# Seven block products in another order: the second layer's down stage of a trunk kernel, with two weight sums by DMA and later weight loads

## The chip, the cores and the metric

The kernel runs on one core of a Trainium2 chip. The metric is the device time of one execution in microseconds. The kernel before was timed three times, the changed kernel is timed beside it.

## The reference

One sequence of 1024 tokens with 1024 channels goes through two layers in fp32. Each layer has a token mixer and a dense FFN, both behind an RMSNorm and an affine modulation, with a gate on the residual; one RMSNorm ends the stack.

```python
for i in range(DEPTH):                       # DEPTH = 2, D_FF = 2816
    mod = c_act @ ada_w[i] + ada_b[i]
    sh_m, sc_m, g_m, sh_f, sc_f, g_f = jnp.split(mod, N_ADA, axis=-1)
    h = modulate(rms_norm(x, norm_mix_g[i]), sh_m, sc_m)
    y = conformer_conv(...) if i % 2 == 0 else multiscale_pool(...)
    x = x + (1.0 + g_m)[:, None, :] * y
    h = modulate(rms_norm(x, norm_ffn_g[i]), sh_f, sc_f)
    y = (silu(h @ w_gate) * (h @ w_up)) @ w_down
    x = x + (1.0 + g_f)[:, None, :] * y
return rms_norm(x, final_g)
```

The change is in the last line but one of the second layer's FFN, the product with `w_down`, and in the final norm.

## The kernel before

**Numbers and tiles.** Activations lie with channels on the 128 partitions and tokens along the free axis, in two chunks A and B of 512 tokens. Every fp32 value is used as a pair of a rounded part and a rest ("hi", "lo"), and every product is three passes on TensorE (hi x hi, hi x lo, lo x hi). So a weight tile that comes in as `raw` needs a cast on ScalarE (`w<-raw`, CAST, the hi) and a subtraction on VectorE (`w<-raw,w`, the lo), and an operand block `op` likewise (`hi<-op`, `lo<-op,hi`). All vector, scalar and POOL arithmetic is recorded at line 126, all matmuls at line 148.

**Stages.** Layer 0 (convolution mixer, FFN), layer 1's pooling mixer, then layer 1's FFN. Gate and up run as eleven joint units (`joint`, line 1176) with one level of Strassen's block scheme: each unit needs sums of weight blocks, which are made by a load on SP (`raw<-in_wgu_dram`) and an accumulating DMA on POOL into the same tile (line 1108), or by subtractions on VectorE (`s<-raw,raw`). At its end a unit writes three operands `k` for the down stage to DRAM (`kinds<-k`, from `paired`, line 1232).

**The down stage** (`Seven`, lines 1480 and following; about 1500 to 1704 us). The product with `w_down` is cut in 2 x 2 blocks and done as seven block products p1 to p7. Each has parts q = 0 to 5, each part one weight tile of 128 x 1024 (q = 5 half as wide) and one operand; a whole part is 24 matmuls of 512 columns. Four PSUM banks gather a block product over its parts. The banks of "x" gather p1, then p6, p7 and p4 on top of it, and at the end of each some half of a chunk is complete and is added to the residual by four VectorE instructions (`x<-dn,gains,x`, the updates, line 1008). The banks of "y" gather p2's parts 4 and 5, and later p5 and p3. (p2's other parts are done elsewhere.) The table's columns are name, weight, operand, banks, whether the banks start fresh, which (chunk, half) is updated at the end, and the parts:

```python
("p2", "a12", "b21", "y", True, [(A, 0)], [4, 5]),
("p1", "a11", "b11", "x", True, [(A, 0)], every),
("p6", "s2", "t2", "x", False, [(B, 0)], every),
```

The weights a12, a11, a22 are plain loads of `in_wds_dram`. s1 and s2 come by a load and an accumulating DMA on POOL. s2 then subtracts a11, which p1 left in the block named `s`. s3 and s4 are a load followed by a subtraction on VectorE (`weights_of`, line 1426, its `load` and `halves`).

**Order.** TensorE's instructions stay in the order of the program. The other engines' and the queues' order is set by a scheduler that goes by its own estimates; an edge such as "behind the products" (`order`, line 150) only fixes a place in the queue and makes nothing wait on the chip. `Seven.run` emits a unit per part: first it loads the part four steps on, then it splits the part two steps on (cast and subtraction), then come the products, then the updates if the step ends. Loads go through SP in order: each part's weight and operand, and each waits for a free slot (five for raw weights, four for operands). The accumulations wait in POOL's queue.

**The end.** p3's last parts run in two halves of 256 token columns (`ending`), in whose shadow the norm of B's first half is made: a sum over partitions by matmuls (`var<-ones,acc`), eight tiny VectorE steps for the inverse root (`col`, `var`), a spread by matmul (`rstd<-ident,col`), scalings of x and output. Chunk A's final norm (`final`, line 1630) is a task that starts when p4 has ended and runs beside p5 and p3.

Of the kernel before, what the change touches and what calls it, by code (L numbers as in the profile page):

```python
# [12 lines left out]
AF = mybir.ActivationFunctionType  # L13
# [50 lines left out]
SPLIT = 2  # L64
# [67 lines left out]
def trunk(ctx, tc, xT, c, vec, ada, adan, w1f, w1, wdg, w2, wgu, wdn, wds, wpl, out):  # L132
# [526 lines left out]
    def unit(emit, *weights):  # L659
        units.append((weights, emit))  # L660
# [515 lines left out]
    def joint(l, fp, between=None):  # L1176
# [55 lines left out]
        def paired(i, f, g, u):  # L1232

            duo, k = kinds_d[l][fp // 2], c.setdefault("k", {})
            if i:
                if not k:
                    k[0] = block("u0", "k", F32)
                else:
                    k[1], k[2] = block("u0", "k", F32), block("u0", "k", F32)
                    sync.dma_start(k[2][:, 1], kept_d[l][fp // 2][:, fp % 2])  # L1240
                gated(l, i, f, g, u, into=k[0][:, 1 - f % 2])
                if 1 in k:
                    V_.tensor_tensor(k[1][:, 0], k[0][:, 1], k[0][:, 0], op=SUB)
            else:
                gated(l, i, f, g, u, into=k[2][:, 0])
                V_.tensor_tensor(k[1][:, 1], k[1][:, 0], k[2][:, 0], op=ADD)
                V_.tensor_tensor(k[2][:, 1], k[2][:, 1], k[1][:, 1], op=SUB)
                V_.tensor_tensor(k[0][:, 0], k[0][:, 1], k[1][:, 1], op=SUB)
                for b in (2, 1, 0):
                    soft.dma_start(duo[b][:, fp % 2], k[b])  # L1250

# [174 lines left out]
    def weights_of(l, kind, q):  # L1426

        n = duo_width(q) * 512
        src = lambda b: wds[q, b][:, :n]
        got = {}  # L1430

        def load():
            if kind == "a11":
                r = st["s2", q] = block("h0", "s", F32).rearrange("p a b -> p (a b)")[:, :n]
            else:
                r = raw_tile()[:, :n]
            first, *plus = {"a11": (0,), "a12": (1,), "a22": (3,), "s1": (2, 3), "s2": (2, 3), "s3": (3,), "s4": (1,)}[kind]
            nc.sync.dma_start(r, src(first))
            for b in plus:
                order(nc.gpsimd.dma_start(r, src(b), accum_op=ADD))  # L1440
                clock["G"] = max(clock["G"], clock["PE"]) + 0.9
            got["raw"] = r

        def halves():
            r = got["raw"]
            if kind in ("s2", "s3", "s4"):
                h = st["s2", q]
                to = r if kind == "s3" else h
                V_.tensor_tensor(to, r, h, op=SUB)
                r = to  # L1450
            wt = wts.tile([P, 2, D], F32R, tag="w", name=nm("w"))
            S_.copy(wt[:, 0, :n], r)
            V_.tensor_tensor(wt[:, 1, :n], r, wt[:, 0, :n].bitcast(F32), op=SUB)
            return wt

        return load, halves
# [23 lines left out]
    class Seven:  # L1480
# [24 lines left out]
        def run(self, after={}, ending=None):  # L1505
            for i, (name, key, fresh, ends, qs, q) in enumerate(self.steps):
                def emit(take, i=i, key=key, fresh=fresh, ends=ends, qs=qs, q=q):
                    self.load(i + LOADED + 1)
                    self.split(i + SPLIT + 1)
                    if key is None:  # L1510
                        return
                    if fresh and q == qs[0]:
                        self.banks[key] = [bank("dn") for _ in range(4)]
                    bs, (wt, ops) = self.banks[key], self.ready.pop(i)
                    for ds in ((0, 1), (2, 3)):
                        for j, g in enumerate(ops):
                            for d in ds:
                                last = q == qs[-1] and j == len(ops) - 1
                                products(bs[d], wt, 4 * j + d, g, fresh and q == qs[0] and j == 0, last, more=True)
                                if last:  # L1520
                                    for ch, half in ends:
                                        update(ch, 4 * half + d, bs[d], gate_f, self.l)
                            pace()
                unit(emit)
                if (name, q) in after:
                    after[name, q]()
            if ending is not None:
                unit(lambda take: ending([self.ready.pop(i) for i in sorted(self.ready)]))
# [99 lines left out]
        return upper, emit  # L1628

    def final(ch):  # L1630
        acc = yield from sum_sq(x[ch.i], ch.n)
        rstd = yield from mean_rsqrt(acc, ch.n, True, loose=True)
        for k in range(KT):
            xs = x[ch.i][k]
            V_.scalar_tensor_tensor(xs, xs, V("final_g", k), rstd, op0=MUL, op1=MUL)
            nc.sync.dma_start(out[:, k, ch.t0 : ch.t0 + ch.n], xs)
            yield
# [266 lines left out]
    def pool_end(ch):  # L1904
# [17 lines left out]
    every = list(range(NQ))  # L1922
    short = [q for q in every if q not in LAST]
    seven = Seven(1, [
        ("p2", "a12", "b21", "y", True, [(A, 0)], [4, 5]),
        ("p1", "a11", "b11", "x", True, [(A, 0)], every),
        ("p6", "s2", "t2", "x", False, [(B, 0)], every),
        ("p7", "s3", "t3", "x", False, [(B, 1)], every),
        ("p4", "a22", "t4", "x", False, [(A, 1)], every),
        ("p5", "s1", "t1", "y", True, [(B, 1)], every),  # L1930
        ("p3", "s4", "b22", "y", False, [(B, 0)], short),
        ("p3", "s4", "b22", None, True, [], LAST),
    ])
    all_joint(1, HEADS[1], between=seven.begin)
    upper, last_part = ending(B, 1)
    seven.run({
        ("p1", 0): lambda: unit(lambda take: x_in(B)),
        ("p4", NQ - 1): lambda: put("final_a", lambda: final(A)),
        ("p5", NQ - 1): lambda: unit(upper),
    }, last_part)  # L1940
    run_units(W_BUFS, early)

# [60 lines left out]
```

## Time and profile before

| | us |
|---|---|
| median of 3 runs | 1721.03 |
| lowest, highest | 1719.14, 1721.04 |
| profiled execution, its own time | 1717.94 |
| its span | 1716.1 |
| TensorE busy | 1676.0 (98%) |
| VectorE busy | 1321.6 (77%) |
| ScalarE busy | 795.3 (46%) |
| POOL busy | 475.7 (28%) |

The granted TensorE clock is 0.994 on average. The profile names instructions by tile (`out<-in`); an idle time in brackets is that of the engine just before the instruction, with what ended it. The profiled execution's own time lies 1.8 us above its span.

### The profile page before, as it was taken

The page shows a single profiled execution, that of the slowest core. Times are in us where ns is not written, and L with a number is a line of the kernel's source. Part 1 is how long each engine was busy: PE and PEld are TensorE (multiplying, and loading weights), DVE is VectorE, ACT ScalarE, POOL GpSimd, SP SyncE. Part 2 cuts the span into 40 slices and gives each one's busy share as a digit, 9 for nine tenths or more (in the row PEclk, how much of TensorE's full clock was granted, in tenths as well). Part 3 has the DMA queues.
Part 4 walks back from the last instruction along what each step waited for, and adds up shares of the span by engine and source line. Part 5 has one row for each costly group of instructions (what it writes and reads, how often), then busy time and mean ns, then how long its engine had stood idle before and what let it go on. Part 6 is the DMA issues. An engine that isn't in the chain of part 4 may idle for free.

```text
span 1716.1 us, 21376 instructions
## 1 busy us (share of the span) xinstructions
PE 1676.0 (98%) x7614; PEld 1362.7 (79%) x7614; DVE 1321.6 (77%) x1879; ACT 795.3 (46%) x1077; POOL 475.7 (28%) x561
## 2 busy tenths in 40 slices
PE   7999999999999999999999999999999999999987
PEld 5777777778887888888888888888788888878877
DVE  8889898898669797877665987868676767685485
ACT  3678686866546233233223437637222222233433
POOL 2588767795001121221110301101111111000101
PEclk9999999999999999999999999999999999999999
DMA  8958997737775888976876748868877777675851
GB/s 303 284 169 238 232 226 200 214 98 215 245 233 135 269 288 262 301 250 240 337 266 224 258 147 240 250 222 222 224 210 221 222 224 216 236 242 171 241 179 53
DMA packets 117613, 386.48 MB, mean 225 GB/s; under 512 B 12481, under 2 KB 14657, under 8 KB 117506
## 3 DMA queue, kind: packets, MB, share of 16 engines
q1 hardware_dynamic: 79680, 253.23, 42.1%
q0 software_dynamic: 36736, 130.83, 31.1%
q8 instruction: 60, 0.98, 0.2%
q10 hardware_dynamic: 1090, 1.05, 0.2%
q14 instruction: 47, 0.39, 0.1%
HBM read 317.69 MB, written 63.18 MB: 222 GB/s over the span
## 4 chain that ended last, share of the span: by engine, by line
PE 83%; DVE 5%; DMA 5%; issue 3%; POOL 1%; ACT 1%; DVEq 0%; POOLq 0%; ACTq 0%
PE dn L148 23%; PE a L148 22%; PE e L148 13%; PE p L148 9%; PE y L148 6%; PE g L148 3%; PE first L148 3%; PE tap L148 2%; DMA raw<-in_wds_dram 2%; DMA rd<-r 1%; POOL pa L126 1%; PE ada L148 1%; DMA s<-in_wds_dram 1%; DMA adaw<-in_adan_dram 1%; DVE t L126 1%
## 5 line engine op out<-in xcount | busy, mean ns | idle before, releaser
L126 ACT CAST w<-raw 128x1024 fp32r<-128x1024 f32 (+1 forms) x249 | 259.0, 1042 | 337.8 <-PE dn L148 97.7
L148 PE MATMUL dn<-g,w 128*128 128x512 f32 x1152 | 265.2, 391 | 1.7 <-DVE g L126 1.0
L126 DVE TENSOR_TENSOR w<-raw,w 128x1024 fp32r<-128x1024 f32 x177 | 217.9, 1234 | 52.7 <-ACT w L126 52.5
L148 PEld LDWEIGHTS dn<-g,w 128*128 128x128 f32 x1152 | 215.7, 188 | 47.6 <-DVE g L126 1.3
L148 PE MATMUL a<-n,w 128*128 128x512 f32 x1056 | 248.0, 390 | 1.2 <-DVE n L126 0.7
L148 PE MATMUL p<-h,w 128*128 128x512 f32 x1056 | 244.5, 391 | 1.7 <-ACT r L126 1.1
L126 POOL TENSOR_TENSOR pa<-pa,pr 128x512 f32<-128x512 f32 x160 | 227.6, 1507 | 23.4 <-ACT pr L126 17.1
L148 PEld LDWEIGHTS a<-n,w 128*128 128x128 f32 x1056 | 197.8, 188 | 44.6 <-DVE n L126 2.2
L148 PEld LDWEIGHTS p<-h,w 128*128 128x128 f32 x1056 | 197.2, 188 | 45.0 <-ACT r L126 2.3
L148 PE MATMUL dn<-hi,w 128*128 128x512 f32 (+1 forms) x600 | 177.4, 378 | 5.3 <-DVE x L126 5.3
L126 DVE SCALAR_TENSOR_TENSOR ca<-u,vecs,ca 128x512 f32<-128x512 f32 x245 | 169.7, 745 | 0.5
L126 DVE SCALAR_TENSOR_TENSOR x<-dn,gains,x 128x512 f32<-128x512 f32 (+1 forms) x140 | 98.4, 730 | 48.6 <-PE dn L148 48.6
L148 PEld LDWEIGHTS dn<-hi,w 128*128 128x128 f32 x600 | 111.0, 191 | 28.3 <-DVE x L126 7.2
L148 PE MATMUL a<-t,w 128*128 128x512 f32 x528 | 126.1, 395 | 4.6 <-DVE w L126 2.9
L148 PE MATMUL e<-b,w 128*128 128x512 f32 x528 | 123.4, 390 | 0.6 <-DVE r L126 0.6
L148 PE MATMUL e<-t,w 128*128 128x512 f32 x528 | 123.3, 389 | 0.0
L148 PEld LDWEIGHTS a<-t,w 128*128 128x128 f32 x528 | 100.5, 191 | 26.8 <-DVE w L126 3.8
L126 ACT ACTIVATE pr<-u,vecs 128x512 f32<-128x512 f32 x160 | 108.2, 716 | 24.3 <-POOL pa L126 18.8
L148 PEld LDWEIGHTS e<-b,w 128*128 128x128 f32 x528 | 99.1, 188 | 21.6 <-DVE r L126 1.0
L148 PEld LDWEIGHTS e<-t,w 128*128 128x128 f32 x528 | 99.1, 188 | 20.5
L1108 POOL DMA_DIRECT2D raw<-in_wgu_dram x41 | 36.3, 885 | 281.7 <-DVE k L126 88.3
L148 PE MATMUL dn<-lo,w 128*128 128x512 f32 (+1 forms) x300 | 112.9, 376 | 0.0
(179 smaller groups left out, 2371.3 us busy)
## 6 DMA issues: line engine op xcount, KB each, us to landing
raw<-in_wgu_dram SPq DMA_DIRECT2D x132, 512.0 KB, 5.1
adaw<-in_ada_dram POOLq DMA_DIRECT2D x48, 512.0 KB, 7.2
raw<-in_wdn_dram SPq DMA_DIRECT2D x44, 512.0 KB, 8.4
raw<-in_wgu_dram POOLq DMA_DIRECT2D x41, 512.0 KB, 7.1
raw<-in_w_dram SPq DMA_DIRECT2D x36, 512.0 KB, 6.3
gd<-g POOLq DMA_DIRECT2D x36, 512.0 KB, 7.8
g<-gd SPq DMA_DIRECT2D x36, 512.0 KB, 5.7
kinds<-k POOLq DMA_DIRECT2D x33, 512.0 KB, 7.2
```

The source lines that it names most:

```text
L126: self.last = self.order(getattr(self.eng, name)(out, *args, **kw))
L148: last_mm[0] = nc.tensor.matmul(out, lhsT, rhs, start=start, stop=stop, skip_group_check=more).ins.name
L1108: d = order(nc.gpsimd.dma_start(w[i], wgu[l, fp, src], accum_op=ADD))
```

## The change

1. The order of the steps. Before: p2, p1, p6, p7, p4, p5, p3. After: p2, p5, p1, p6, p7, p4, p3. p2 now gathers in "x" and p5 in "y" right behind it, and p5 serves both halves of B at its end (eight updates). p3 starts its banks afresh.
2. The sign of the operand t2 and of the weight sum s2 is turned. In `paired` two subtractions become additions and one addition becomes a multiply-and-subtract. s3 and s4 can then be sums: s3 is A22 loaded, with s2 accumulated by a POOL DMA from SBUF; s4 is A12 accumulated in place on s2 by a POOL DMA. Twelve VectorE subtractions go, and six more accumulating DMAs come.
3. All loads and accumulations of `in_wds_dram` get the edge behind the last product emitted (`placed`).
4. Chunk B's x is loaded block by block, one behind each of p5's first four parts. On the last part of a step the next split is emitted behind the updates.
5. Chunk A's final norm starts behind p7 with four of its squares; the rest waits until p4 has ended. The squares of B's upper half come behind p7 too.

```diff
-                V_.tensor_tensor(k[1][:, 1], k[1][:, 0], k[2][:, 0], op=ADD)
-                V_.tensor_tensor(k[2][:, 1], k[2][:, 1], k[1][:, 1], op=SUB)
-                V_.tensor_tensor(k[0][:, 0], k[0][:, 1], k[1][:, 1], op=SUB)
+                V_.scalar_tensor_tensor(k[1][:, 1], k[1][:, 0], -1.0, k[2][:, 0], op0=MUL, op1=SUB)
+                V_.tensor_tensor(k[2][:, 1], k[2][:, 1], k[1][:, 1], op=ADD)
+                V_.tensor_tensor(k[0][:, 0], k[0][:, 1], k[1][:, 1], op=ADD)
...
+        def placed(d):
+            if last_mm[0] is not None:
+                tc.add_manual_dep(d.ins, last_mm[0], edge, reason="behind the products")
+
+        def plus(r, what):
+            placed(nc.gpsimd.dma_start(r, what, accum_op=ADD))
+            clock["G"] = max(clock["G"], clock["PE"]) + 0.9
+
         def load():
+            if kind == "s4":
+                got["raw"] = st["s2", q]
+                plus(st["s2", q], src(1))
+                return
...
+            placed(nc.sync.dma_start(r, src({"a11": 0, "a12": 1, "a22": 3, "s1": 2, "s2": 2, "s3": 3}[kind])))
+            if kind in ("s1", "s2"):
+                plus(r, src(3))
+            elif kind == "s3":
+                plus(r, st["s2", q])
...
-            if kind in ("s2", "s3", "s4"):
+            if kind == "s2":
                 h = st["s2", q]
-                to = r if kind == "s3" else h
-                V_.tensor_tensor(to, r, h, op=SUB)
-                r = to
+                V_.tensor_tensor(h, h, r, op=SUB)
+                r = h
...
                     self.load(i + LOADED + 1)
-                    self.split(i + SPLIT + 1)
+                    if key is None or q != qs[-1]:
+                        self.split(i + SPLIT + 1)
...
+                    self.split(i + SPLIT + 1)
...
     def final(ch):
-        acc = yield from sum_sq(x[ch.i], ch.n)
+        acc = temp(ch.n, "acc", 2)
+        for k in range(KT):
+            while k == KT // 2 and "a_done" not in st:
+                yield "wait"
...
-        ("p2", "a12", "b21", "y", True, [(A, 0)], [4, 5]),
+        ("p2", "a12", "b21", "x", True, [(A, 0)], [4, 5]),
+        ("p5", "s1", "t1", "y", True, [(B, 1), (B, 0)], every),
...
-        ("p1", 0): lambda: unit(lambda take: x_in(B)),
-        ("p4", NQ - 1): lambda: put("final_a", lambda: final(A)),
-        ("p5", NQ - 1): lambda: unit(upper),
+        **{("p5", m): lambda m=m: unit(lambda take: x_in(B, m)) for m in range(KT // 2)},
+        ("p7", NQ - 1): final_begins,
+        ("p4", NQ - 1): lambda: unit(lambda take: st.__setitem__("a_done", True)),
```

**Place 1: POOL's queue at the start of the second layer's joint stage.** The difference of the two orders; `raw_12285`, `raw_12321` and `raw_12357` are weights of p6, the others belong to the joint stage and its normed inputs.

```order
 L488 DMA w_9751<-in_wgu_dram 128x1024
-L1440 DMA raw_12285<-in_wds_dram 128x1024
 L1096 DMA w_9852<-raw_9842 128x1024
-L1440 DMA raw_12321<-in_wds_dram 128x1024
 L165 DMA kept_4_203<-t_9880 128x512
-L1440 DMA raw_12357<-in_wds_dram 128x1024
 L165 DMA kept_4_203<-t_9947 128x512
 L1096 DMA w_9919<-raw_9844 128x1024
```

The three accumulations stood between the joint stage's own; now none of the down stage's is here. On SP the five loads that stood here (these three and p2's two) are gone as well.

**Place 2: weights that need a load and an accumulation.** SP's queue before, at p5's loads (`raw_12909` to `raw_13017` are the weights of p5's parts 0 to 3, `op_12912` to `op_12984` its operands 0 to 2, `op_12876` is p4's last operand):

```order
L1438 DMA raw_12909<-in_wds_dram 128x1024
L158 DMA op_12876<-kinds_5_2_222 128x512
L1438 DMA raw_12945<-in_wds_dram 128x1024
L158 DMA op_12912<-kinds_0_0_205 128x2x512
L1438 DMA raw_12981<-in_wds_dram 128x1024
L158 DMA op_12948<-kinds_1_0_208 128x2x512
L1438 DMA raw_13017<-in_wds_dram 128x1024
L158 DMA op_12984<-kinds_2_0_211 128x2x512
```

SP's queue now, at p7's loads (`raw_12713` to `raw_12823` are the weights of its parts 0 to 3, `op_12753` to `op_12854` its operands 1 to 4):

```order
L158 DMA op_12753<-kinds_1_1_209 128x2x512
L1449 DMA raw_12713<-in_wds_dram 128x1024
L158 DMA op_12790<-kinds_2_1_212 128x2x512
L1449 DMA raw_12750<-in_wds_dram 128x1024
L158 DMA op_12826<-kinds_3_1_215 128x2x512
L1449 DMA raw_12787<-in_wds_dram 128x1024
L158 DMA op_12854<-kinds_4_1_218 128x2x512
L1449 DMA raw_12823<-in_wds_dram 128x1024
```

A weight of part n stood behind the operand of part n-2; now it stands behind that of part n+1. VectorE's order now at the end of p6 (`w_12792`, `w_12844`, `w_12856` are the low halves of p7's weights 0 to 2; `dn_12438` to `dn_12441` are p6's four banks):

```order
L126 TENSOR_TENSOR w_12792<-raw_12713,w_12792 128x1024
L126 TENSOR_TENSOR lo_12796<-op_12716,hi_12795 128x1024
L126 TENSOR_TENSOR w_12844<-raw_12750,w_12844 128x1024
L126 TENSOR_TENSOR lo_12848<-op_12753,hi_12847 128x1024
L126 TENSOR_TENSOR w_12856<-raw_12787,w_12856 128x1024
L126 SCALAR_TENSOR_TENSOR x_12247<-dn_12438,gains,x_12247 128x512
L126 TENSOR_TENSOR lo_12860<-op_12790,hi_12859 128x1024
L126 SCALAR_TENSOR_TENSOR x_12247<-dn_12439,gains,x_12247 128x512
```

Before, the same rows stood there in the same way, but with weights that were one load each and a subtraction. The updates stand behind the low half of the next step's third weight in both.

**Place 3: VectorE at the end.** Now (`var_13541` and `col_13544` are the root of the ending's first half, `ny_13566` is A's spread root, `x_12285<-dn_13580` and `x_12285<-dn_13606` are the last two updates):

```order
L126 SCALAR_TENSOR_TENSOR var_13541<-col_13544 128x2
L126 SCALAR_TENSOR_TENSOR x_10797<-x_10797,vecs,ny_13566 128x512
L126 SCALAR_TENSOR_TENSOR x_10989<-x_10989,vecs,ny_13566 128x512
L126 SCALAR_TENSOR_TENSOR x_11181<-x_11181,vecs,ny_13566 128x512
L126 SCALAR_TENSOR_TENSOR col_13544<-var_13541,col_13544 128x2
L126 SCALAR_TENSOR_TENSOR x_10989<-x_10989,vecs,ny_13566 128x512
L126 SCALAR_TENSOR_TENSOR x_11181<-x_11181,vecs,ny_13566 128x512
L126 SCALAR_TENSOR_TENSOR x_10797<-x_10797,vecs,ny_13566 128x512
L126 SCALAR_TENSOR_TENSOR x_11373<-x_11373,vecs,ny_13566 128x512 x2
L126 SCALAR_TENSOR_TENSOR x_12285<-dn_13580,gains,x_12285 128x256
```

Before, the same place held only the root's steps and the last two updates (`x_12244<-dn_13588` and the next); A's eight scalings stood inside p3's first parts.

More of the change, by code (lines that the diff above doesn't have):

```diff
@@ L1436, in load @@
                 r = raw_tile()[:, :n]
[L1437 to L1441, printed above, removed]
+            placed(nc.sync.dma_start(r, src({"a11": 0, "a12": 1, "a22": 3, "s1": 2, "s2": 2, "s3": 3}[kind])))
[3 more added lines that the diff above has]
+                plus(r, st["s2", q])
             got["raw"] = r
@@ L1630, in final @@
     def final(ch):
-        acc = yield from sum_sq(x[ch.i], ch.n)
+        acc = temp(ch.n, "acc", 2)
+        for k in range(KT):
+            while k == KT // 2 and "a_done" not in st:
+                yield "wait"
+            sq = temp(ch.n) if k else acc
+            S_.activation(sq, x[ch.i][k], AF.Square)
+            if k == KT - 1:
+                V_.scalar_tensor_tensor(acc, sq, EPS_SUM, acc, op0=ADD, op1=ADD)
+            elif k:
+                V_.tensor_tensor(acc, acc, sq, op=ADD)
+            yield
         rstd = yield from mean_rsqrt(acc, ch.n, True, loose=True)
@@ L1929, in trunk @@
         ("p4", "a22", "t4", "x", False, [(A, 1)], every),
-        ("p5", "s1", "t1", "y", True, [(B, 1)], every),
-        ("p3", "s4", "b22", "y", False, [(B, 0)], short),
+        ("p3", "s4", "b22", "y", True, [(B, 0)], short),
         ("p3", "s4", "b22", None, True, [], LAST),
@@ L1935, in trunk, with final_begins @@
     upper, last_part = ending(B, 1)
+    def final_begins():
+        put("final_a", lambda: final(A))
+        unit(upper)
     seven.run({
-        ("p1", 0): lambda: unit(lambda take: x_in(B)),
-        ("p4", NQ - 1): lambda: put("final_a", lambda: final(A)),
-        ("p5", NQ - 1): lambda: unit(upper),
+        **{("p5", m): lambda m=m: unit(lambda take: x_in(B, m)) for m in range(KT // 2)},
+        ("p7", NQ - 1): final_begins,
+        ("p4", NQ - 1): lambda: unit(lambda take: st.__setitem__("a_done", True)),
     }, last_part)
```

## The prediction

> **What bounds the kernel now.** I read the page's first part, then a table of stretches, then the idle times of TensorE (PE) in the timeline, then what VectorE (DVE) and the DMAs did just ahead of each.
>
> ```profile
> PE 1676.0 (98%) x7614; PEld 1362.7 (79%) x7614; DVE 1321.6 (77%) x1879; ACT 795.3 (46%) x1077; POOL 475.7 (28%) x561
> ```
>
> TensorE is the bound. The change takes no product away, so it can only win where TensorE stands idle or runs at a lower clock, and lose where it makes such places. The stretches (columns: from:to, length, busy time and count of PE, PEld, DVE, ACT, POOL, granted clock, DMA share, GB/s):
>
> ```profile
> 1220.00:1250.00 30.00, 26.05 (x105) 20.77 (x104) 25.32 (x30) 9.66 (x11) 2.54 (x4) 0.89 0.70 218
> 1250.00:1280.00 30.00, 30.00 (x134) 24.86 (x133) 21.30 (x27) 8.12 (x9) 4.31 (x6) 1.00 0.74 210
> 1510.00:1515.00 5.00, 2.26 (x10) 1.43 (x8) 5.00 (x6) 3.91 (x5) 0.00 (x0) 0.96 0.85 294
> 1515.00:1520.00 5.00, 4.53 (x15) 3.25 (x14) 5.00 (x7) 0.94 (x1) 0.88 (x1) 0.70 0.82 248
> 1545.00:1550.00 5.00, 5.00 (x24) 4.12 (x23) 4.01 (x5) 1.34 (x2) 0.00 (x0) 1.00 0.39 138
> 1655.00:1660.00 5.00, 4.11 (x18) 3.45 (x19) 3.30 (x11) 0.00 (x0) 0.00 (x0) 0.79 0.30 105
> 1660.00:1665.00 5.00, 5.00 (x25) 4.21 (x24) 1.33 (x2) 1.57 (x2) 0.00 (x0) 0.86 0.00 0
> ```
>
> An undisturbed stretch does 134 products in 30 us, 0.224 us each, and 24 of them, one part of the down stage, in 5.4 us. TensorE's idle times, in brackets with the releaser:
>
> ```profile
> 1223.59 0.73 PE L148 MATMUL a<-t,w 128*128 128x512 f32 x2 [1.73 <-ACT w L126]
> 1226.54 7.46 PE L148 MATMUL a<-t,w 128*128 128x512 f32 x22 [2.22 <-DVE w L126]
> 1514.18 0.50 PE L148 MATMUL dn<-hi,w 128*128 128x512 f32 x1 [2.74 <-DVE x L126]
> 1515.98 0.79 PE L148 MATMUL dn<-hi,w 128*128 128x512 f32 x1 [0.47 <-DVE x L126]
> 1639.01 0.50 PE L148 MATMUL dn<-hi,w 128*128 128x512 f32 x1 [1.45 <-DVE x L126]
> 1655.89 1.05 PE L148 MATMUL var<-ones,acc 128*128 128x1 f32 x8 [2.31 <-DVE acc L126]
> 1672.51 0.47 PE L148 MATMUL dn<-hi,w 128*128 128x512 f32 x1 [0.62 <-DVE x L126]
> ```
>
> The first two are in the joint gate/up stage, the others in the second layer's down stage: the end of p2, the end of p4, the final norm of chunk A inside p5, and p5's end. The stretches add what the lower clock cost behind them.
>
> **The four waits of the down stage.** *End of p2.* DVE's timeline, then the chain of waits:
>
> ```profile
> 1506.50 1.22 DVE L126 TENSOR_TENSOR w<-s,w 128x1024 fp32r<-128x1024 f32 x1 [3.69 <-ACT w L126]
> 1513.38 0.75 DVE L126 SCALAR_TENSOR_TENSOR x<-dn,gains,x 128x512 f32<-128x512 f32 x1
> 1494.48 14.51 DMA s<-in_wds_dram
> ```
>
> The x update that frees the banks stood from 1511 to 1513.38 behind p1's weight work, which came late because its load took 14.51 us. The stall cost 2.74 + 0.47 us idle, plus 5 x (0.04 + 0.30) = 1.7 us of clock: 4.9. Counted the other way, 14 + 9 products missing against 24 per stretch, 23 x 0.224 = 5.2. I take 5.0. After the change p2 is followed by p5, which writes into fresh banks of its own, so TensorE need not wait for the x updates there until p1, six parts later. What remains is the third p5 weight, w_12212, queued on DVE ahead of p2's updates, and its load plus accumulation fall into DMAs that are still full. That costs 0 (the four x blocks of B no longer load here) to 3 (loads as slow as above); I take 0.5.
>
> *End of p4* (old place of the subtractions for s4):
>
> ```profile
> 1631.72 1.23 DVE L126 TENSOR_TENSOR s<-raw,s 128x1024 f32<-128x1024 f32 x1 [3.60 <-DMA raw<-in_wds_dram]
> 1636.47 1.23 DVE L126 TENSOR_TENSOR s<-raw,s 128x1024 f32<-128x1024 f32 x1 [0.32 <-DMA raw<-in_wds_dram]
> 1638.21 0.74 DVE L126 SCALAR_TENSOR_TENSOR x<-dn,gains,x 128x512 f32<-128x512 f32 x1
> ```
>
> The subtractions wait for their load, and the updates stand behind them. With s4 summed by DMA they are gone, and the step behind p4 is now p3 with weights long loaded: 1.5 us gained. In all, twelve subtractions leave DVE (ten of 1.23, two half as wide, about 13.6 us busy), but DVE is at 77% and elsewhere this is off the path: 0. The turned sign swaps one DVE form for another of nearly the same length, 0.
>
> *Final norm of A in p5.* Its matmuls stood in TensorE's order before their sum was ready: 2.31 us idle, 5 x (0.21 + 0.14) = 1.75 us of clock, 0.35 for the var matmuls themselves: 4.4. They now stand inside the ending, where the squares are long done: 4.4 gained. *1672.51*: the updates stood behind A's eight scalings; these move: 0.6. Together 5.0 + 1.5 + 4.4 + 0.6 = **11.5 gained**.
>
> *A rule against this arithmetic.* The rows show a granted clock of 0.70 and 0.79 behind idle times of 2.74 and 2.31 us. The Trainium skill ("TensorE: Matmul & The Clock Gate", Part 1) puts the drop behind an idle window of about 3.4 us. By that rule no clock would come back or be lost: 3.2 + 1.5 + 2.3 + 0.6 = 7.6 gained here, some 2.5 in the joint stage, 5.9 and 3.7 lost below, a net of -0.5 us, 1720.5. The granted clocks in these rows do not agree, so it gets no chance of its own beside R2, which ends near it, and I keep 11.5.
>
> **The joint stage.** Loads and accumulations of wds are now queued behind products, so three accumulations leave POOL's queue around 1177 to 1199, and five loads leave SP's. What followed there, on DVE and in the chain:
>
> ```profile
> 1210.93 10.23 DMA raw<-in_wgu_dram
> 1221.19 1.23 DVE L126 TENSOR_TENSOR s<-raw,raw 128x1024 f32<-128x1024 f32 x1 [4.88 <-DMA raw<-in_wgu_dram]
> ```
>
> DVE waited 4.88 us for an accumulation that POOL could issue only at 1210.93 and that took 10.23 us; TensorE then lost 1.73 + 2.22 idle and 30 x 0.11 = 3.3 of clock, 7.2 (by count 29 x 0.224 = 6.5; I say 7). Without the three transfers ahead of it I expect it 3 to 5 us earlier, with 4 needed. Range 0 to 7, taken **4.5 gained**. Those loads land in the down stage instead, where they are priced next.
>
> **New waits at the ends of p1 and p6.** p6 and p7 now both need a load and then an accumulation for every weight. SP's queue now has the load of part n behind the operand of part n+1, which waits for the lo of part n-3 to free its slot (before, p5's load stood behind the operand of part n-2). At the end of p1 and of p6, the x updates stand on DVE behind the weight of the next step's third part, so a late weight holds TensorE there. Nothing in the trace is exactly this; p5 before shows the pieces (DVE, SPq, SPq, POOL):
>
> ```profile
> 1606.94 1.22 DVE L126 TENSOR_TENSOR lo<-op,hi 128x1024 fp32r<-128x1024 f32 x1
> 1608.19 0.53 SPq L158 DMA_DIRECT2D op<-kinds  x1
> 1609.32 0.33 SPq L1438 DMA_DIRECT2D raw<-in_wds_dram  x1
> 1616.84 0.86 POOL L1440 DMA_DIRECT2D raw<-in_wds_dram  x1 [1.55 <-DVE lo L126]
> ```
>
> lo to operand 1.25 us, operand to load 1.13, then the latency L of load and accumulation, then the cast and the low half, 1.04 and 1.23 by the rows of the page and of DVE: three parts take 4.6 + L at least, and TensorE takes 3 x 5.4 = 16.3 for them. L has these bounds (the DMAs of 1540 to 1590 and of 1599 to 1630, and the page's):
>
> ```profile
> L126 ACT CAST w<-raw 128x1024 fp32r<-128x1024 f32 (+1 forms) x249 | 259.0, 1042 | 337.8 <-PE dn L148 97.7
> raw<-in_wds_dram SPq DMA_DIRECT2D x5, 512.0 KB, 5.1
> raw<-in_wgu_dram POOLq DMA_DIRECT2D x41, 512.0 KB, 7.1
> raw<-in_wds_dram SPq DMA_DIRECT2D x5, 512.0 KB, 7.4
> raw<-in_wds_dram POOLq DMA_DIRECT2D x5, 512.0 KB, 9.1
> 1599.00:1629.00 30.00, 30.00 (x133) 24.60 (x132) 14.72 (x16) 12.33 (x15) 4.32 (x5) 1.00 0.98 264
> ```
>
> Calm, L = 5.1 + 7.1 + 0.5 (POOL's issue behind the landing) = 12.7: 17.3 against 16.3, 1 us per three parts. Loaded, as in p5 before at a DMA share of 0.98, L = 17: 21.6 against 16.3, 5.3 per three parts. Up to p7's third part there are nine parts, three such rounds: 3 to 16 us, plus about 1.7 of clock per long stall. Fewer transfers are in flight now than in that p5, since loads are issued later, so I take the quarter next to calm, L = 13.5: 1.8 x 3 + about 1.1 of clock = 6.5, nearly all at the end of p6. Range 0 to 19. With the 0.5 from above, **7.0 lost**.
>
> One sentence by a page: the Trainium skill ("DMA: Bandwidth & Descriptors", Anatomy of one DMA) fits a POOL-issued DMA as 2.0 us plus its bytes at 436 GB/s, an estimate of 3.2 us for 512 KB, with which L would be 8.8 and this loss zero. The 7.1 and 9.1 of the trace do not agree with it.
>
> **The tail.** A's eight scalings now stand on DVE inside the root of the ending's first half and ahead of the last two x updates. TensorE runs that half's rstd before the last half's var.
>
> ```profile
> 1665.70 5.39 DVE L126 SCALAR_TENSOR_TENSOR x<-x,vecs,ny 128x512 f32<-128x512 f32 x8 [0.21 <-ACT ny L126]
> 1704.14 0.48 DVE L126 SCALAR_TENSOR_TENSOR x<-dn,gains,x 128x256 f32<-128x256 f32 x1 [1.67 <-PE dn L148]
> 1708.12 0.68 PE L148 MATMUL rstd<-ident,col 128*128 128x128 f32 x4 [1.74 <-DVE col L126]
> ```
>
> They cost 5.39 us; DVE's idle 1.67 ahead of the last update covers a part: **3.7 lost**, between 2.5 (more gaps are used) and 5.4 (none is). In the middle of a step, where they were, they cost only the 0.6.
>
> **Sum.** -11.5 - 4.5 + 7.0 + 3.7 = -5.3 us. The profiled execution took 1717.94 us (span 1716.1), 3.1 below the median of 1721.03, so its own time would become 1712.6, and on the median's scale **1715.7**.
>
> **Rivals.** *R1, the loads keep up* (L below 11.7, so 4.6 + L stays under 16.3, and the whole 7 of the joint stage comes back): -11.5 - 7 + 3.7 = -14.8, 1706.2. For it: 1545 to 1550 has a DMA share of only 0.39. Against: an accumulation took 7.1 even at the usual load. The page's fit for POOL's DMAs would lead here. Chance 0.20.
>
> *R2, the gains are eaten* (the accumulation of 1210.93 still lands late, since four copies with accumulation stay ahead of it on POOL, and L is 14: 2.3 x 3 + 1.7 + 0.5 = 9.1): -11.5 + 9.1 + 3.7 = +1.3, 1722.3. For it: 10.23 us for that one transfer is little touched by what POOL did 12 us earlier. Against: the loads that shared the engines are gone too. Chance 0.17.
>
> *R3, slower* (chained weights run at p5's latencies, L = 17: 16 us at the ends of p1 and p6, two clock drops 3.4, 0.5): -11.5 - 4.5 + 19.9 + 3.7 = +7.6, 1728.6. It decides against the change from 4.6 + L = 19.7, L about 15. For it: p6 and p7 now move a load, an operand and an accumulation per part, just as the 0.98 stretch does. Against: in that stretch TensorE stayed 30.00 of 30.00 us busy, and a stalled TensorE lets the transfers catch up. Chance 0.17.
>
> **How the numbers follow.** About 0.2% (3.4 us) can be told from no change, so faster means below 1717.6 and slower above 1724.5. The forecast's case (1711 to 1719) has 0.46, of which 0.39 is faster and 0.07 within. Faster: 0.39 + 0.20 = 0.59; same: 0.07 + 0.17 = 0.24; slower: 0.17. The range leaves out the half of R1 below 1706 and the half of R3 above 1728: 1706 to 1728. The likeliest case's own range is 1711 to 1719.
>
> **What would show it.** Right: no idle time of PE at p2's end, behind p4 and inside the down stage's last third; A's scalings as rows near the end, the last x update some 4 us behind its products and the last rstd some 4 us behind that update, as now; PE waiting for x at the end of p6 for 3 to 5 us, with DVE waiting for a DMA into raw ahead of it; 1220 to 1250 with over 120 products. Wrong: accumulations in p6 and p7 that land in under 6 us (R1), 1220 to 1250 still with some 105 (R2), or several stalls of over 4 us with loads and accumulations of 7 and 9 us (R3). A stall in p5's first parts would say that the weight sums can't follow p2 that fast.

## The result and the profile after

The changed kernel takes 1729.87 us (median of 4 runs, 1729.20 to 1731.55), the kernel before 1720.22 (1719.14 to 1721.04) beside it: a ratio of 1.0058, 95% interval 1.0041 to 1.0075. It is slower by 10 us, where 5 us less was forecast, and above the range of 1706 to 1728. The profiled execution took 1729.20 us, its span 1727.2, 11.1 more than before.

TensorE's work is the same, and so it is only where it stands still that has changed. The page's line, then five stretches:

```profile
PE 1678.7 (97%) x7614; PEld 1364.6 (79%) x7614; DVE 1311.0 (76%) x1871; ACT 795.7 (46%) x1077; POOL 484.2 (28%) x573
```
```profile
1220.00:1250.00 30.00, 30.00 (x134) 24.80 (x133) 26.40 (x33) 10.53 (x12) 3.35 (x5) 1.00 0.62 200
1570.00:1575.00 5.00, 1.41 (x3) 0.83 (x3) 3.81 (x5) 2.94 (x3) 0.86 (x1) 0.55 0.97 215
1575.00:1580.00 5.00, 4.92 (x18) 3.82 (x18) 4.78 (x6) 1.05 (x1) 0.00 (x0) 0.77 0.89 236
1610.00:1615.00 5.00, 4.45 (x10) 3.11 (x11) 5.00 (x7) 1.34 (x2) 0.75 (x1) 0.52 1.03 177
1645.00:1650.00 5.00, 4.43 (x11) 3.05 (x12) 2.54 (x3) 1.91 (x3) 0.00 (x0) 0.55 1.02 386
```

The joint stage is whole again, 134 products where there were 105. Three stretches of the down stage do 3 to 11 products where 24 fit. TensorE's idle times there, in its timeline:

```profile
1508.92 0.50 PE L148 MATMUL dn<-hi,w 128*128 128x512 f32 x1 [1.41 <-DVE x L126]
1573.59 0.77 PE L148 MATMUL dn<-hi,w 128*128 128x512 f32 x1 [6.12 <-DVE x L126]
1610.47 0.77 PE L148 MATMUL dn<-hi,w 128*128 128x512 f32 x1 [4.72 <-DVE x L126]
1645.06 0.47 PE L148 MATMUL dn<-hi,w 128*128 128x512 f32 x1 [2.12 <-DVE x L126]
```

These are the ends of p2, p1, p6 and p7. Summing by how much the start-to-start times of the down stage's products exceed their usual 0.2265 us gives what each place cost, clock included, and I use this count from here on. The sixteen small products of A's norm, which both kernels run, are left out of it:

| us lost | p2's end | p5's end | p1's end | p6's end | p7's end | p4's end | A's norm | sum |
|---|---|---|---|---|---|---|---|---|
| before | 5.1 | 0.9 | - | - | - | 1.7 | 4.2 | 11.9 |
| after | 2.8 | - | 8.3 | 7.3 | 6.3 | - | - | 24.7 |

From its first to its last product the down stage takes 203.4 us before (1500.4 to 1703.8) and 215.5 after (1496.5 to 1712.0), 12.1 more; 24.7 - 11.9 is 12.8. From the last product to the end it was 12.3 us and is 15.2. The joint stage brought 7 us; in this profiled execution 3 of them were lost again at 1131 us, where TensorE waited 2.1 us for ScalarE (0.9 before) and ran at a granted clock of 0.80 to 0.85 for the next few us. In the experiments' profiles with the same edge the down stage starts at 1493.1 to 1494.5.

**The wait at p1's end, followed back.** VectorE, SP's and POOL's queue of the changed kernel, then the DMAs of 1545 to 1605:

```profile
1564.61 1.23 DVE L126 TENSOR_TENSOR w<-s,w 128x1024 fp32r<-128x1024 f32 x1 [1.19 <-ACT w L126]
1569.15 1.22 DVE L126 TENSOR_TENSOR s<-s,raw 128x1024 f32<-128x1024 f32 x1 [2.18 <-DMA raw<-in_wds_dram]
1571.56 1.23 DVE L126 TENSOR_TENSOR w<-s,w 128x1024 fp32r<-128x1024 f32 x1 [1.19 <-ACT w L126]
1572.70 0.74 DVE L126 SCALAR_TENSOR_TENSOR x<-dn,gains,x 128x512 f32<-128x512 f32 x1
```
```profile
1550.23 0.55 SPq L1449 DMA_DIRECT2D raw<-in_wds_dram  x1
1558.93 0.87 POOL L1437 DMA_DIRECT2D raw<-in_wds_dram  x1 [1.36 <-DMA raw<-in_wds_dram]
```
```profile
raw<-in_wds_dram SPq DMA_DIRECT2D x9, 512.0 KB, 7.8
raw<-in_wds_dram POOLq DMA_DIRECT2D x5, 512.0 KB, 7.5
raw<-s POOLq DMA_DIRECT2D x3, 512.0 KB, 8.1
```

p1's last product began at 1567.1. Its updates stood behind the low half of p6's third weight (1571.56), whose load was issued at 1550.23, whose accumulation at 1558.93, and which could be used at 1569.15: L = 18.9 us. The five whole weights of p6 took 13.8, 14.9, 18.9, 17.5 and 11.7 us from load to landing, 15.4 in the mean. TensorE itself did not need the third weight yet: the low half of the second was done at 1565.8 and that of the third at 1572.8, and without the wait p6's second part would have begun at about 1572.8 and its third at 1578.2 (parts of 5.4 us behind 1567.3).

**The wait at p7's end** was not foreseen. Here p4's weights are single loads. POOL's queue, ScalarE and VectorE, and the DMAs of 1620 to 1642:

```profile
1620.40 2.12 POOL L1437 DMA_DIRECT2D s<-in_wds_dram  x2
1624.13 0.88 POOL L1437 DMA_DIRECT2D s<-in_wds_dram  x1 [1.61 <-PE dn L148]
1630.53 0.86 POOL L1437 DMA_DIRECT2D s<-in_wds_dram  x1 [5.53 <-issue]
```
```profile
1640.54 1.05 ACT L126 CAST w<-raw 128x1024 fp32r<-128x1024 f32 x1 [4.90 <-DMA raw<-in_wds_dram]
1641.62 1.23 DVE L126 TENSOR_TENSOR w<-raw,w 128x1024 fp32r<-128x1024 f32 x1 [4.72 <-ACT w L126]
1642.76 1.48 DVE L126 TENSOR_TENSOR acc<-acc,t 128x512 f32<-128x512 f32 x2
1644.16 0.74 DVE L126 SCALAR_TENSOR_TENSOR x<-dn,gains,x 128x512 f32<-128x512 f32 x1
```
```profile
s<-in_wds_dram POOLq DMA_DIRECT2D x5, 512.0 KB, 9.8
raw<-in_wds_dram SPq DMA_DIRECT2D x4, 512.0 KB, 13.4
```

All six accumulations of s4, not needed before p3, went out between 1620 and 1637. Beside them p4's plain loads took 13.4 us where such loads took 5.1 in the calm stretch of the kernel before, and p7's updates stood behind the low half of p4's third weight (1641.62) and two additions of A's norm.

**The tail.** VectorE at the end:

```profile
1708.65 2.07 DVE L126 SCALAR_TENSOR_TENSOR x<-x,vecs,ny 128x512 f32<-128x512 f32 x3
1710.71 3.39 DVE L126 SCALAR_TENSOR_TENSOR x<-x,vecs,ny 128x512 f32<-128x512 f32 x5
1714.02 0.47 DVE L126 SCALAR_TENSOR_TENSOR x<-dn,gains,x 128x256 f32<-128x256 f32 x1
```

A's scalings keep the last two updates until 1714.02, 2 us behind the last product's start at 1712.0.

### The profile page after: what moved, and what is told of

It reads as the page before. It is cut to its first block, busy times and chain, and to the rows that moved or that the text cites. A ratio compares the mean times of both kernels' runs of the same rounds, so it can differ in the third digit from the quotient of the medians.

```text
span 1727.2 us, 21380 instructions
## 1 busy us (share of the span) xinstructions
PE 1678.7 (97%) x7614; PEld 1364.6 (79%) x7614; DVE 1311.0 (76%) x1871; ACT 795.7 (46%) x1077; POOL 484.2 (28%) x573
## 3 DMA queue, kind: packets, MB, share of 16 engines
q10 hardware_dynamic: 1090, 1.05, 0.2%
## 5 line engine op out<-in xcount | busy, mean ns | idle before, releaser
L126 POOL TENSOR_TENSOR pa<-pa,pr 128x512 f32<-128x512 f32 x160 | 229.5, 1521 | 23.0 <-ACT pr L126 16.6
```

The lines of the kernel that those rows point to most:

```text
L126: self.last = self.order(getattr(self.eng, name)(out, *args, **kw))
```

## The experiments

**Theory 1:** the down stage's waits come from the place of the weight loads in SP's queue. The edge behind the products puts part n's load behind the operand of part n+1, so it starts only when a slot is freed that late, and load, accumulation, cast and low half no longer fit. **Theory 2, the rival:** the DMA engines are full there (0.89 to 1.03 in the stretches above), and a load lands late wherever it stands. The kernel before, run beside the experiments, took 1717.9 to 1719.4 (medians). What tells the theories apart is less the time than where it is lost:

| us lost | time | ratio to before, interval | p2's end | p5's end | p1's end | p6's end | p7's end |
|---|---|---|---|---|---|---|---|
| changed kernel | 1729.9 | 1.0058, 1.0041 to 1.0075 | 2.8 | - | 8.3 | 7.3 | 6.3 |
| weights first | 1718.2 | 0.9997, 0.9986 to 1.0007 | - | - | 10.2 | 1.3 | 3.9 |
| updates first | 1730.5 | 1.0064, 1.0041 to 1.0086 | 0.9 | - | 9.7 in p6 | 2.7 | 11.5 |
| free loads | 1719.7 | 0.9998, 0.9988 to 1.0008 | - | 7.3 | 0.2 | 0.2 | 0.2 |
| norm sooner | 1726.5 | 1.0043, 1.0027 to 1.0060 | 2.4 | - | 9.6 | 2.2 | 11.1 |
| one mark | 1715.6 | 0.9985, 0.9976 to 0.9994 | 5.0 | 6.1 | 0.2 | 0.2 | 0.2 |
| one mark, norm | 1710.9 | 0.9960, 0.9946 to 0.9973 | 4.0 | 7.0 | 0.2 | 0.2 | 0.2 |
| s3 on VectorE | 1719.5 | 1.0008, 0.9999 to 1.0017 | 1.8 | - | 9.2 | 6.4 | 0.7 |
| lag 1, norm | 1713.9 | 0.9976, 0.9967 to 0.9985 | - | - | 10.4 | 1.5 | 3.9 |
| lag 2, norm | 1710.2 | 0.9954, 0.9937 to 0.9972 | 1.0 | - | 10.1 | 0.2 | 0.2 |
| lag 3, norm | 1716.3 | 0.9988, 0.9977 to 1.0000 | 6.2 | - | 12.0 | 0.2 | 0.2 |
| lag 2, norm, in turn | 1703.5 | 0.9919, 0.9904 to 0.9933 | 1.0 | - | 0.2 | 2.5 | 0.2 |

0.2 is the usual seam between two steps.

**Weights first.** Each weight one part ahead of its operand in the program.

```diff
         def load(self, upto):
+            while self.weights < min(upto + 1, len(self.parts)):
+                self.parts[self.weights][0][0]()
+                self.weights += 1
             while self.loads < min(upto, len(self.parts)):
-                for part in self.parts[self.loads]:
-                    part[0]()
+                self.parts[self.loads][1][0]()
                 self.loads += 1
```

> The changed kernel with each part's weight load emitted one part ahead of its operand, so that on SP the weight of part n stands behind the operand of part n, not n+1. Theory 1 (the loads stand too late in SP's queue, and the x updates on VectorE stand behind the weight that comes late): loads and accumulations start about 5.4 us earlier, the idle times of 6.1 us at the end of p1 and 4.7 us at the end of p6 shrink to under 1 us each and the low clock behind them (3.4 us each) goes; about 12 to 17 us less than the changed kernel's 1729.9, so 1713 to 1718. Theory 2 (the DMA engines are full there, wherever a load stands): the loads start earlier and land at the same time, both idle times stay within 1.5 us of what they were, 1727 to 1731.

1718.2 us, 12 less and at the upper edge of theory 1's 1713 to 1718. The ends of p6 and p7 give 8.4 of it, p2's end 2.8 and an earlier start of the down stage 2. p1's end cost 1.9 more, against the expectation; why, the lags below show.

**Updates first.** p6's subtractions and every weight's low half behind the last updates emitted.

```diff
             V_.tensor_tensor(wt[:, 1, :n], r, wt[:, 0, :n].bitcast(F32), op=SUB)
+            if "updated" in st:
+                tc.add_manual_dep(V_.last.ins, st["updated"], edge, reason="behind the updates")
...
                                         update(ch, 4 * half + d, bs[d], gate_f, self.l)
+                                        st["updated"] = V_.last.ins.name
```

> The changed kernel with the weights' low halves that are split at a step's end ordered on VectorE behind that step's x updates. Theory 1: the updates no longer wait for a late weight; the idle times at the ends of p1, p6 and p7 (6.1, 4.7 and 2.1 + 0.5 us) go or fall under 1 us, since the third weight is needed only two parts (10.9 us) later; 1708 to 1716. Theory 2 (the weights come too late for TensorE itself, the updates' place only shows it): TensorE waits about as long inside the next step, for w instead of x; 1725 to 1731.

No gain, and the wait changed its name. TensorE, inside p6:

```profile
1576.31 1.22 PE L148 MATMUL dn<-hi,w 128*128 128x512 f32 x2 [7.79 <-DVE w L126]
```

ScalarE and VectorE ahead of it:

```profile
1565.45 2.19 ACT L126 CAST w<-s 128x1024 fp32r<-128x1024 f32 x2 [2.17 <-DVE s L126]
```
```profile
1564.15 2.35 DVE L126 TENSOR_TENSOR s<-s,raw 128x1024 f32<-128x1024 f32 x2
1568.73 1.23 DVE L126 TENSOR_TENSOR s<-s,raw 128x1024 f32<-128x1024 f32 x1 [2.23 <-DMA raw<-in_wds_dram]
1573.89 1.23 DVE L126 TENSOR_TENSOR s<-s,raw 128x1024 f32<-128x1024 f32 x1 [2.80 <-DMA raw<-in_wds_dram]
1575.03 2.36 DVE L126 TENSOR_TENSOR w<-s,w 128x1024 fp32r<-128x1024 f32 x2
```

The number is what theory 2 forecast, but the rows do not bear it out. p6's second and third weight had landed and were cast by 1567.6, before TensorE came to a stand at 1568.5. Their low halves (1575.03) stood on VectorE behind the subtractions of the fourth and fifth weight, which waited for their accumulations. So the edit put the wait in another place of VectorE's order, and the run tells nothing against theory 1 at p1's end.

**Free loads.** No edge at all.

```diff
         def placed(d):
-            if last_mm[0] is not None:
-                tc.add_manual_dep(d.ins, last_mm[0], edge, reason="behind the products")
+            return d
```

> The changed kernel without the edge of the weight loads and accumulations behind the products: SP and POOL take them as early as the scheduler likes. If the edge alone keeps the joint stage free, 1220 to 1250 falls back from 134 products to about 105 (7 us lost there). Theory 1: p6's and p7's loads stand earlier, so the idle times at the ends of p1 and p6 shrink by 3 us or more each with the clock behind them; 1717 to 1725 in all. Theory 2: those idle times stay, 1734 to 1738.

This tells the theories apart. The stretch of p1's end, of this kernel and then of the changed one:

```profile
1560.00:1580.00 20.00, 20.00 (x89) 16.30 (x88) 10.58 (x12) 8.02 (x8) 5.54 (x7) 1.00 1.06 282
1220.00:1250.00 30.00, 25.93 (x103) 20.60 (x103) 25.42 (x30) 9.45 (x11) 2.54 (x4) 0.89 0.70 214
```
```profile
1560.00:1580.00 20.00, 13.80 (x53) 10.49 (x53) 13.03 (x13) 5.99 (x6) 1.73 (x2) 0.83 0.91 220
```

The DMA engines are fuller (1.06 against 0.91) and TensorE does not wait: theory 2 falls. The joint stage is back at 103 products, so the edge alone had freed it, and the edge alone makes the three waits of the down stage.

**Norm sooner.** A's sum over partitions 3 us instead of 8 behind its squares, by the program's clock.

```diff
-        rstd = yield from mean_rsqrt(acc, ch.n, True, loose=True)
+        rstd = yield from mean_rsqrt(acc, ch.n, True, when="settled", loose=True)
```

> The changed kernel with chunk A's final sum taken to TensorE 3 us instead of 8 us behind its squares by the program's own clock, so that A's eight scalings come in the ending's first half. Theory of the tail (eight scalings, 5.4 us, between the last half's root steps and its last two updates): the time from the last product to the end falls from 15.2 to about 12.3 us as before the change, 1727 in all. Rival (they only move to another place that TensorE waits for, or the longer tail has another cause): 1729 to 1731.

3.4 us less than the changed kernel; from the last product to the end it takes 12.4 us. The tail's term is shown to be A's scalings. At p7's end TensorE here waited 8.9 us for the cast of p4's weight itself, so there the loads were late for TensorE too, and not only for the updates.

**One mark.** The edge of all loads behind one product, the last ahead of the down stage's first load.

```diff
-                tc.add_manual_dep(d.ins, last_mm[0], edge, reason="behind the products")
+                tc.add_manual_dep(d.ins, st.get("mark", last_mm[0]), edge, reason="behind the products")
...
             def emit(take):
+                st["mark"] = last_mm[0]
                 self.load(LOADED)
```

> The changed kernel with the edge of every weight load and accumulation of the down stage at one place only, the last product before the stage's first load, so that loads cannot slip into the joint stage but stand as early as the scheduler likes behind it. Theory 1 (the queue place of the loads made the waits): 134 products in 1220 to 1250 as after the change, and no idle time of PE over 1 us at the ends of p1, p6 and p7, as without any edge; at most the 2.8 and 1.9 us at p5's end stay that the kernel without the edge had. 1719.7 less the 7 of the joint stage: 1711 to 1714. Theory 2 (some of that kernel's calm came from the loads that it had brought in before 1220): the stalls come back in part, 1716 to 1722.

The same with the edit of the norm sooner:

> The same, with A's final sum taken 3 us behind its squares instead of 8, so that A's eight scalings come in the ending's first half. If the tail and the waits are separate terms, another 3 us less than with one mark alone: 1708 to 1711, below both kernels. If the scalings only fill a gap that the other waits had left: within 1 us of one mark alone.

Both points of theory 1 hold: 133 and 134 products in 1220 to 1250, no wait at the ends of p1, p6 and p7, at a DMA share of 1.05 in 1560 to 1580. The time is 2 us over the forecast, since the waits at p2's and p5's ends cost 11.1. With A's norm sooner it takes 4.7 us less and beats both kernels. p5's end looks like the price of too early weights; TensorE with one mark:

```profile
1537.22 0.80 PE L148 MATMUL dn<-hi,w 128*128 128x512 f32 x1 [2.76 <-ACT hi L126]
```

It waits for an operand: eleven weight loads now stand ahead of it on SP.

**Before with one mark.** The same edge in the kernel before, nothing else.

```diff
-            nc.sync.dma_start(r, src(first))
+            placed(nc.sync.dma_start(r, src(first)))
             for b in plus:
-                order(nc.gpsimd.dma_start(r, src(b), accum_op=ADD))
+                placed(nc.gpsimd.dma_start(r, src(b), accum_op=ADD))
```

> The kernel before with only that one-place edge added, no other part of the change. If the joint stage's 7 us were lost to the down stage's loads and accumulations ahead of it on the queues, as read from the trace, 1220 to 1250 does 134 products and the time falls by 5 to 7 us, 1712 to 1715, with the 2.7 us idle at p2's end larger or equal since its weights come no earlier. Rival: the time comes back at p2's end, where three more weights then load into full DMAs; 1717 to 1721.

1717.1 us, ratio 0.9990 (0.9981 to 1.0000). The joint stage does its 134 products, but p2's end costs 7.8 instead of 5.1 (and p1's end 2.2):

```profile
1507.57 0.80 PE L148 MATMUL dn<-hi,w 128*128 128x512 f32 x1 [4.13 <-ACT w L126]
```

The rival was right for the larger part: the loads taken out of the joint stage land just ahead of p2's end instead, and beside them p1's five whole loads took 19.8 us in the median (13.4 before).

**s3 on VectorE.** s3 by an addition on VectorE again; the loads keep their places.

```diff
-            elif kind == "s3":
-                plus(r, st["s2", q])
...
+            elif kind == "s3":
+                V_.tensor_tensor(r, r, st["s2", q], op=ADD)
```

> The changed kernel with s3 summed on VectorE again (an addition, since the sign is turned) and not by a DMA: p7's chain loses its accumulation, its loads stand in the same places of SP's queue. Theory 1 (the loop from a freed operand slot over load, accumulation, cast and low half, 4.6 + L for three parts of 16.3 us): with L about 6 to 8 for a load alone p7 keeps up; the 4.7 us idle at p6's end and 3.4 us of clock go, the 6.1 us at p1's end stay; 1720 to 1724. Theory 2 (the place alone decides, or full DMAs): the idle time at p6's end stays over 3 us, 1727 to 1731.

The time is half a us below theory 1's range, but the place is not as it had it: p6's end still costs 6.4, with 3.1 us idle. VectorE there:

```profile
1601.75 1.22 DVE L126 TENSOR_TENSOR raw<-raw,s 128x1024 f32<-128x1024 f32 x1 [1.46 <-DMA raw<-in_wds_dram]
1602.89 0.74 DVE L126 SCALAR_TENSOR_TENSOR x<-dn,gains,x 128x512 f32<-128x512 f32 x1
1604.69 1.22 DVE L126 TENSOR_TENSOR raw<-raw,s 128x1024 f32<-128x1024 f32 x1
```

The additions for p7's fourth and fifth weight stand ahead of and between the updates, and the fourth still waits for its load, so a link less in the chain helped little at p6's end while the loads kept their place. What went is p7's end (0.7), and s4's accumulations ran at other times: two of the six went out before 1592 and the last at 1617.4. In this run p4's loads issued from 1612 to 1623, beside the other four, took 13.0 us, and the whole loads issued from 1595 to 1612, before these went out, 5.0.

**Lags.** All three with the norm sooner. The edge of a part's load goes to the product emitted one, two or three parts earlier, which moves the weight of part n behind the operand of part n, n-1 or n-2.

```diff
+                marks = st.get("marks", [last_mm[0]])
-                tc.add_manual_dep(d.ins, last_mm[0], edge, reason="behind the products")
+                tc.add_manual_dep(d.ins, marks[max(0, len(marks) - 1 - 2)], edge, reason="behind the products")
...
+                    st["marks"].append(last_mm[0])
                     self.load(i + LOADED + 1)
```

> The changed kernel with A's sum taken sooner, and with the edge of a weight's load behind the products of one part earlier: on SP the weight of part n stands behind the operand of part n, whose slot the lo of part n-4 frees. Theory 1 (a loop: freed slot, load, accumulation, cast, low half; 4.6 + L must fit into the parts between): four parts are 21.8 us, 4.6 + L about 18 to 23 with the L of 14 to 19 that the changed kernel showed, so part of the waits stays, above all at p1's end: some 8 us of the 24 in the down stage, 1710 to 1716. Theory 2 (full DMAs): all of it stays, 1724 to 1728.

> The same with the edge two parts earlier: the weight of part n stands ahead of the operand of part n and behind that of part n-1, freed by the lo of part n-5. Theory 1: five parts are 27.2 us, more than 4.6 + L; no idle time of PE over 1 us at the ends of p1, p6 and p7; the operands are not pushed back as they are without the step-wise edge, so the wait at p5's end (4.3 to 6 us there) is under 3; 1705 to 1709. Theory 2: 1724 to 1728. If the waits at p5's end come from the accumulations of p5 itself and not from the operands' place, it stays: 1709 to 1712.

> The same with the edge three parts earlier: behind the operand of part n-2, as p5's loads stood before the change. Theory 1: nothing more to win at the ends of p1, p6 and p7; within 2 us of the two-part lag, either way.

At the ends of p6 and p7 the loss goes 2.2 and 11.1 (no lag), 1.5 and 3.9, 0.2 and 0.2, 0.2 and 0.2: with the place, as theory 1 has it. At lag 2 p4's loads still took 16.6 us beside those accumulations, and TensorE did not wait for them. p1's end stays at 10 to 12 in all, where the expectation for lag 2 had no wait, so its time came 1.2 us above the range; lag 1 came into its range though it lost 15.8 us in these places, not some 8. Lag 3 loses 6 us at p2's end again, so earlier is not better everywhere; the forecast for it missed by 4 us. VectorE at p1's end with lag 2:

```profile
1564.86 1.23 DVE L126 TENSOR_TENSOR s<-s,raw 128x1024 f32<-128x1024 f32 x1 [8.24 <-DMA raw<-in_wds_dram]
1568.27 1.22 DVE L126 TENSOR_TENSOR s<-s,raw 128x1024 f32<-128x1024 f32 x1
1569.41 0.74 DVE L126 SCALAR_TENSOR_TENSOR x<-dn,gains,x 128x512 f32<-128x512 f32 x1
```

Here the first two weights were done by 1556.6 and the third was cast by 1556.8. Its low half stood behind the subtraction of the fourth, and p1's updates behind those of the fourth and fifth.

**Lag 2, norm, in turn.** p6's subtractions each behind the weight before it and behind the last updates.

```diff
                 V_.tensor_tensor(h, h, r, op=SUB)
+                for name in {st["in_turn"], st["updated"]}:
+                    tc.add_manual_dep(V_.last.ins, name, edge, reason="in turn")
```

> The two-part lag with A's sum sooner, and on VectorE p6's subtractions in turn: each behind the low half of the weight before it and behind the last updates emitted. The two-part lag alone still waited 7.2 us at p1's end, where its trace has VectorE at the subtractions of p6's fourth and fifth weight (one of them 8.2 us idle for its accumulation) ahead of p1's updates. Theory 1a (there the place of the updates behind weights that TensorE does not need yet makes the wait): the 7.2 us and about 2.7 us of clock go, less up to 2 us because the second weight's low half comes just in time; 1701 to 1704. Theory 1b (the weights are too late for TensorE there as well, as in the changed kernel with its updates first): TensorE waits as long for w one to three parts later; 1708 to 1712.

1703.5 us, 0.8% below the kernel before. All of the down stage's waits for x together, by the sums of waits from 1485 on (total, times, longest):

```profile
PE dn L148 <- DVE x L126: 2.7, 3, 1.2
```

The wait at p1's end is gone and no wait for a weight came in its place. So with lag 2 it was the order on VectorE, the updates and low halves behind subtractions that wait for an accumulation, that made it. The same order without the lag was not run.

## Why the prediction was wrong

**What held.** The waits that were to go went: 11.9 us by the count, 11.5 forecast. The joint stage gave 7 (4.5 forecast, range 0 to 7), shown by the free loads to come from the edge. The tail cost 2.9 (3.7), shown by the norm sooner. That the drop of the clock counts beside the idle time held too: behind 6.12 and 4.72 us idle the stretches grant 0.55 and 0.52. So did the weighing of the clock rule in the Trainium skill ("TensorE: Matmul & The Clock Gate", Part 1): 0.55 also follows 2.12 us idle at p7's end, under its 3.4.

**What failed** is the step "I take the quarter next to calm, L = 13.5", and with it the term of 7.0 us lost, which measured 24.7. Its reason, that fewer transfers would be in flight, hardly held: the DMA share from 1545 to 1605 is 0.87, near the 0.98 of the loaded stretch and far from the 0.50 of the calm one. L was 15.4 in the mean over p6. Put into the prediction's own formula, 4.6 + 15.4 - 16.3 = 3.7 per three parts and 11.1 for three rounds; the idle times at the ends of p1 and p6 are 6.1 + 4.7 = 10.8. That they agree so closely is partly luck: the 4.6 leaves out p6's subtraction between landing and cast (1.22 in the row at 1569.15), and nearly all of the wait was forecast for p6's end, while more than half of it came at p1's. The form of the loop was right and its size was not. The rest of the 24.7: clock behind these two waits, about 4.8 (1.1 forecast); p2's end 2.8 (0.5); and p7's end 6.3, which no case had. It stands outside that formula: plain loads that were needed ran beside accumulations that nobody needed yet, and took 13.4 us. No run moved these accumulations alone, so that they slowed the loads is argued from the times, but the lags show that loads as slow do no harm when they start earlier.

**The rival R3** forecast 1728.6 and came within 1.3 us, but not by its own sum: it had 16 us idle at the ends of p1 and p6, where 10.8 came, and none at p7's end. Its condition (4.6 + L over 19.7) was met by the mean (20.0).

**The updates' place.** The prediction named the updates behind the third weight as what makes the wait. The rows bear this out at p1's end, where TensorE did not yet need that weight. At lag 2, where it was the fourth and fifth, changing the order took the wait away. That updates first moved no time is no evidence against it, since that edit held up the low halves instead. What the prediction did not ask is how late the loads had to be: the edge that freed the joint stage and the edge that delayed p6's and p7's loads are the same line, and it priced the two as separate terms.

**Still open.** Whether the order on VectorE alone, without a lag, would free p1's and p6's ends, why TensorE lost up to 3 us at 1131 in some profiles, why lag 3 loses at p2's end, and whether the order of the steps alone gains anything, which wasn't tried without the other parts.

## What to carry to other kernels

A queue place tied to the products is right as a lower bound ("not before this stage") and harmful as a pace: where a weight needs a load and an accumulation, count the parts between the event that frees its queue and its use, and leave the measured latency under load, not the calm one. When an engine waits for an update, look at what stands ahead of the update and ask whether that was late for the end consumer too; moving the update first can answer it in one run, if what then stands ahead of the late consumer's input is looked at too. A transfer that nobody needs yet may not be free: here the loads beside such transfers took 13 us, not 5.

## What the runs showed of the hardware

A 512 KB load by SP took 5.1 us in the calm stretch of the kernel before (DMA share 0.50), 7.8 with accumulations beside it (0.87) and 13.4 beside six POOL accumulations (1.01; the whole ones took 9.8), all medians. Accumulations out of SBUF (`raw<-s`, 8.1) were no quicker in the same stretch than those out of DRAM (7.5); the Trainium skill's fit for POOL-issued DMAs ("DMA: Bandwidth & Descriptors", Anatomy of one DMA), an estimate of 3.2 us, agrees with neither. Full DMA engines did not by themselves hold TensorE: at a share of 1.06 it stayed busy 20.00 of 20.00 us.
